# A hybrid decoder layer on one core: two token tiles come channel-major by layout, and the small constants come in three arrays

## The chip, the cores and the metric

The kernel runs on one core of one Trainium2 chip. A core has a matrix engine (TensorE, PE in the profile, with its weight loads shown as PEld), a vector engine (VectorE, DVE), a scalar engine (ScalarE, ACT), GpSimd (POOL) and SyncE (SP), which here issues most of the DMA transfers. The metric is the device time of one execution in microseconds, lower is better; times before are the median of 3 runs.

## The reference, cut to what matters

One decoder layer over 512 tokens of 1024 channels: a root-mean-square norm, a projection to queries, keys, values, a gated convolution's input and two gates, sliding-window attention, the convolution module, a merge, and a squared-ReLU MLP with 4096 hidden channels.

```python
def rms_norm(x, g):
    xf = x.astype(jnp.float32)
    y = xf * lax.rsqrt(jnp.mean(xf * xf, axis=-1, keepdims=True) + EPS)
    return (y * g.astype(jnp.float32)).astype(x.dtype)
...
        u = rms_norm(x, norm_mix_g[l])
        proj = u @ w_in[l]
        q = proj[..., :Q_END].reshape(b, s, N_Q_HEADS, HEAD_DIM)
        k = proj[..., Q_END:K_END].reshape(b, s, N_KV_HEADS, HEAD_DIM)
        v = proj[..., K_END:V_END].reshape(b, s, N_KV_HEADS, HEAD_DIM)
        glu_in = proj[..., V_END:GLU_END]
...
        attn = sliding_window_attention(q, k, v, attn_sinks[l], rel_bias) @ w_attn_o[l]
        conv = conformer_conv(glu_in, w_dw[l], b_dw[l], conv_ln_g[l], conv_ln_b[l], w_conv_out[l])
        merged = jax.nn.sigmoid(gate_attn) * attn + jax.nn.sigmoid(gate_conv) * conv
        x = x + merged @ w_out[l]
        hmid = jnp.square(jax.nn.relu(rms_norm(x, norm_mlp_g[l]) @ w_ff1[l]))
        x = x + hmid @ w_ff2[l]
```

The change concerns the first norm, `u`, and how the small constants (the norm gains of q and k, the sinks, the bias buckets, the convolution's taps, bias and norm) reach the chip.

## The kernel before

Every product is made of three matmuls in a reduced format: each operand is split into a high part (ACT casts it) and a low part (DVE or POOL subtracts the high part from the original), and high times high, high times low and low times high are summed in PSUM. All products need the activations with channels on partitions, so `u` is kept as `uTh` and `uTl`, 128 channels by 8 groups by 512 tokens.

The 512 tokens are four tiles of 128. For each tile the start of the program does this: SP loads x with tokens on partitions; ACT squares it with a running sum and takes the root (`x_square`, L294 to L297); DVE makes the reciprocal with one correction step (`rsqrt_root`, L125 to L131) and scales x by it and by the gain `gmix` in one pass (`x_scale`, L300); PE transposes the result in eight 128x128 pieces through the identity into two PSUM banks (`x_trans`, which calls `transpose_split`, L201); from each bank ACT casts the high part (L209) and DVE subtracts for the low part (L210). Then come the tile's k projection (`k_proj`) and v projection (`v_proj`), each 16 matmuls with the high weights (L316, L317) and 8 with the low ones (L320), with ACT evacuating k and its squares (L279, L281), and ACT and DVE splitting v (L333, L335). PSUM has two banks in turn for these sums (tag `mm`), two for transposes (tag `tr`) and two of tag `s`.

The order of all this is written out by hand at the end of the function (the block under `manual_schedule`): each engine executes its instructions in the order in which they stand there, and waits at an instruction whose operands are not ready with everything behind it queued. Between the tiles the first two weight chunks of the convolution's input are split (`split_hi` on ACT, L462; `split_lo` on POOL, L466). What comes after is a list of events with due positions, sorted once; `columns` (at position -2) is its first.

`columns` takes the convolution's constants: 34 rows of 1024 (31 taps, bias, norm gain, norm bias) loaded as rows, transposed on PE in eight pieces into one PSUM bank (L361), then copied on DVE to `wcol`, one column of 34 per channel and group, with the taps and the norm constants halved. It also makes the table of the relative bias with one small matmul (L363). The small constants come with nine loads of their own, issued by SP after the four tiles of x (L257 to L265).

[...] `raw_g` and `raw_a` are the first weight chunks of the convolution's input, in two buffers taken over from the raw weights of k and v.

Of the kernel before, what the change touches and what calls it, by code (L numbers as in the profile page):

```python
# [53 lines left out]
def tile_hybrid_block(  # L54
    ctx: ExitStack,
    tc: tile.TileContext,
    x: bass.AP,
    norm_mix_g: bass.AP,
    w_in: bass.AP,
    q_norm_g: bass.AP,  # L60
    k_norm_g: bass.AP,
    attn_sinks: bass.AP,
    rel_bias: bass.AP,
    w_attn_o: bass.AP,
    w_dw: bass.AP,
    b_dw: bass.AP,
    conv_ln_g: bass.AP,
    conv_ln_b: bass.AP,
# [5 lines left out]
    onehot: bass.AP,  # L74
# [24 lines left out]
    def bc(ap, n):  # L99
        return ap.partition_broadcast(n)  # L100
# [156 lines left out]
    nc.sync.dma_start(gq, bc(q_norm_g[0], P))  # L257
# [6 lines left out]
    nc.sync.dma_start(rb, rel_bias)
    nc.sync.dma_start(oh, onehot)  # L265
# [28 lines left out]
    def x_square(t, ss):  # L294
        us[t] = att.tile([P, D], F32, name=f"u_{t}", tag="pt", bufs=3)
        se.activation(us[t], xt[t], AF.Square, accum_out=ss)
        se.activation(root[t], ss, AF.Sqrt, scale=1.0 / D, bias=epsc)  # L297
# [54 lines left out]
    NR = CW + 3  # L352
    wcol = whole_lines(keep, P, KD * NR, "wcol").rearrange("p (k n) -> p k n", n=NR)
# [4 lines left out]
    def columns():  # L358
        wc_ps = ps1.tile([P, KD, NR], F32, name="wc_ps", tag="s")
        for k in range(KD):  # L360
            pe.transpose(wc_ps[:, k, :], rows[0:NR, k * P:(k + 1) * P], ident[0:NR, 0:NR])  # L361
# [3 lines left out]
        ve.tensor_copy(wcol, wc_ps)  # L365
# [1094 lines left out]
```

## Time and profile before

| | |
|---|---|
| median of 3 runs | 758.08 us (757.91 to 758.11) |
| the profiled execution | 757.91 us, its span 756.1 us |
| granted TensorE clock | 0.999 |
| PE busy | 750.6 us (99% of the span), 4474 instructions |
| DVE busy | 606.0 us (80%) |
| ACT busy | 441.3 us (58%) |
| POOL busy | 273.4 us (36%) |
| the first weights' products after the norm (`ps_g`) start | 38.10 us |

The span runs from the first to the last instruction; the measured time is 1.8 us longer. A row of a timeline or chain gives the start, the length, and the line with its operation; "x8" means eight records merged into one row; an f32 matmul that is not a transpose leaves two records. "[1.70 <-PE tp_u L207]" is idle time of that engine ahead of the row and what ended it.

### The profile page before, as it was taken

How to read it: one execution, taken by the hardware profiler on the slowest of the kernel's cores; microseconds unless marked ns; L12 is line 12 of the kernel's file. 1: busy time of each engine (PE TensorE's matmuls, PEld its weight loads, DVE VectorE, ACT ScalarE, POOL GpSimd, SP SyncE). 2: the span in 40 equal slices, each digit the busy share in tenths (PEclk: the TensorE clock that was granted, in tenths of full speed). 3: DMA queues.
4: the chain of work that ended last, by engine and by line, in shares of the span. 5: the costliest groups of instructions: out<-in, count | busy, mean ns of one | idle time of the engine just before them, and what ended most of it. 6: DMA issues, size and time to landing. Idle time of an engine off the chain costs nothing.

```text
span 756.1 us, 11678 instructions
## 1 busy us (share of the span) xinstructions
PE 750.6 (99%) x4474; PEld 663.6 (88%) x4474; DVE 606.0 (80%) x928; ACT 441.3 (58%) x697; POOL 273.4 (36%) x214
## 2 busy tenths in 40 slices
PE   9999999999999999999999999999999999999997
PEld 8989989898888888888888899988998899889986
DVE  5466998789878988878346679899879987998795
ACT  7445457757666665339235357864676467636861
POOL 1453968948774566443531002210121012101210
PEclk9999999999999999999999999999999999999999
DMA  7441040312314113531338205983498349834772
GB/s 262 149 161 56 1 168 15 126 56 81 115 61 137 56 55 112 168 111 56 112 111 294 97 29 91 263 198 117 127 230 200 112 123 228 203 116 115 171 162 111
DMA packets 66014, 97.48 MB, mean 129 GB/s; under 512 B 3540, under 2 KB 36612, under 8 KB 65958
## 3 DMA queue, kind: packets, MB, share of 16 engines
q1 hardware_dynamic: 56710, 78.91, 31.2%
q0 software_dynamic: 9248, 17.83, 13.4%
q8 instruction: 35, 0.57, 0.3%
q14 instruction: 21, 0.17, 0.1%
HBM read 94.60 MB, written 2.12 MB: 128 GB/s over the span
## 4 chain that ended last, share of the span: by engine, by line
PE 98%; DVE 2%; issue 0%; POOL 0%; DVEq 0%; POOLq 0%
PE ps_x L1177 12%; PE ps_z L1182 12%; PE ps_y L1182 6%; PE ps_y L1177 6%; PE ps_z L1177 3%; PE ps_x L1182 3%; PE ps_g L498 2%; PE ps_q L197 2%; PE ps_q L198 2%; PE ps_q L199 2%; PE ps_a L498 2%; PE ps_ta L498 2%; PE ps_a L500 2%; PE ps_g L500 2%; PE ps_g L499 2%; PE ps_ta L500 2%
## 5 line engine op out<-in xcount | busy, mean ns | idle before, releaser
L1148 DVE TENSOR_TENSOR piecel<-block,pieceh 128x1024 fp32r<-128x1024 f32 x112 | 135.7, 1219 | 27.8 <-ACT pieceh L1145 27.6
L1145 ACT CAST pieceh<-block 128x1024 fp32r<-128x1024 f32 x112 | 116.7, 1050 | 67.5 <-DVE block L1138 21.7
L803 DVE SCALAR_TENSOR_TENSOR cv<-h,wcol,cv 128x512 f32<-128x512 f32 x208 | 146.2, 746 | 0.5
L1124 POOL DMA_DIRECT2D block<-in_w_ff_dram x34 | 41.3, 1241 | 287.3 <-DVE piecel L1148 157.1
L1177 PE MATMUL ps_x<-xSh,pieceh 128*128 128x256 f32 x192 | 53.0, 276 | 0.0
L1177 PE MATMUL ps_x<-xSl,pieceh 128*128 128x256 f32 x192 | 53.0, 276 | 0.0
L1177 PE MATMUL ps_x<-xSh,piecel 128*128 128x256 f32 x192 | 53.0, 276 | 0.0
L711 ACT ACTIVATE s<-s,negm 128x257 f32<-128x257 f32 (+1 forms) x64 | 30.4, 479 | 16.0 <-DVE negm L703 16.0
L1182 PE MATMUL ps_z<-piecel,aSh 128*128 128x512 f32 (+1 forms) x98 | 37.9, 387 | 0.0
L1182 PE MATMUL ps_z<-pieceh,aSh 128*128 128x512 f32 (+1 forms) x98 | 37.7, 385 | 0.0
L1182 PE MATMUL ps_z<-pieceh,aSl 128*128 128x512 f32 (+1 forms) x98 | 37.7, 385 | 0.0
L1138 DVE TENSOR_TENSOR block<-block,block 128x1024 f32<-128x1024 f32 x30 | 36.5, 1221 | 0.8 <-DMA block<-in_w_ff_dram 0.4
L795 POOL TENSOR_TENSOR side<-side,tap 128x512 f32<-128x512 f32 x24 | 31.2, 1298 | 15.1 <-ACT tap L794 15.1
L197 PE MATMUL ps_q<-wh_q,uTh 128*128 128x256 f32 x128 | 36.5, 285 | 0.0
L199 PE MATMUL ps_q<-wh_q,uTl 128*128 128x256 f32 x128 | 36.2, 283 | 0.0
L198 PE MATMUL ps_q<-wl_q,uTh 128*128 128x256 f32 x128 | 36.2, 283 | 0.0
L1177 PEld LDWEIGHTS ps_x<-xSh,piecel 128*128 128x128 f32 x192 | 36.0, 188 | 0.0
L1177 PEld LDWEIGHTS ps_x<-xSh,pieceh 128*128 128x128 f32 x192 | 36.0, 188 | 0.0
L1177 PEld LDWEIGHTS ps_x<-xSl,pieceh 128*128 128x128 f32 x192 | 36.0, 188 | 0.0
L735 DVE TENSOR_TENSOR pTl<-ptp,pTh 128x512 fp32r<-128x512 f32 x28 | 19.0, 686 | 17.8 <-ACT pTh L731 17.8
L720 POOL TENSOR_TENSOR s<-s,r 128x1024 f32<-128x1024 f32 (+1 forms) x16 | 26.9, 1684 | 16.7 <-DVE r L715 16.7
L1216 ACT CAST aSh<-c 128x1024 fp32r<-128x1024 f32 x16 | 16.8, 1053 | 21.4 <-DVE c L1230 11.7
(325 smaller groups left out, 2531.8 us busy)
## 6 DMA issues: line engine op xcount, KB each, us to landing
block<-in_w_ff_dram SPq DMA_DIRECT2D x64, 512.0 KB, 5.5
block<-in_w_ff_dram POOLq DMA_DIRECT2D x34, 512.0 KB, 6.9
x<-in_x_dram SPq DMA_DIRECT2D x8, 512.0 KB, 4.2
raw_g<-in_w_in_dram SPq DMA_DIRECT2D x8, 512.0 KB, 4.4
raw_a<-in_w_in_dram SPq DMA_DIRECT2D x8, 512.0 KB, 3.5
raw_q<-in_w_in_dram SPq DMA_DIRECT2D x8, 512.0 KB, 4.5
raw_ta<-in_w_in_dram SPq DMA_DIRECT2D x8, 512.0 KB, 4.3
raw_tc<-in_w_in_dram SPq DMA_DIRECT2D x8, 512.0 KB, 3.5
```

What stands on the lines that cost most here:

```text
L197: pe.matmul(ps, ah, wh, start=first, stop=False)
L198: pe.matmul(ps, ah, wl, start=False, stop=False)
L199: pe.matmul(ps, al, wh, start=False, stop=last)
L498: pe.matmul(ps, wh[:, k, :], ah(k), start=(k == 0), stop=False)
L500: pe.matmul(ps, wl[:, k, :], ah(k), start=False, stop=(k == KD - 1))
L803: ve.scalar_tensor_tensor(out=cps[ct], in0=src, scalar=w, in1=cps[ct], op0=ALU.mult, op1=ALU.add)
L1124: ge.dma_start(tl["raw"][buf][:, ks, :], block(ph, i, j)[:, ks, :], accum_op=ALU.add)
L1138: ve.tensor_tensor(out=o, in0=a, in1=b, op=ALU.add)
L1145: se.copy(piece("h", n), tl["raw"][buf][:, 2 * h:2 * h + 2, :])
L1148: ve.tensor_tensor(out=piece("l", n), in0=tl["raw"][buf][:, 2 * h:2 * h + 2, :], in1=piece("h", n).bitcast(F32), op=ALU.subtract)
L1177: pe.matmul(o, b[:, c, w], a[:, k, :], start=(first and c + q + i == 0), stop=(k == 3 and i == 2), skip_group_check=True)
L1182: pe.matmul(acc[:, cols], a[:, k, w], b[:, c, cols], start=(first and c + i == 0), stop=(k == 3 and i == 2), skip_group_check=True)
```

## The change

Four things change.

1. Token tiles 2 and 3 are loaded twice. The host lays out a second copy of these 256 tokens, `x_cols`, with 128 channels on partitions and 8 groups by 128 tokens behind each. The token-major copy is now only squared and summed (in place); the other one, `xc`, becomes `u`: DVE multiplies by the gain, which lies one per channel and group in `gcol` (`cols_gain`); PE spreads the tokens' 128 reciprocal roots to all partitions with one f32 matmul per tile (`cols_spread`: the factors as a broadcast stationary operand, the identity as the moving one) into `rsb`; DVE multiplies by `rsb` in two halves into PSUM; ACT casts each half to the high part and DVE subtracts for the low part (`cols_split`). Tiles 0 and 1 go on as before.
2. The convolution's constants and `gcol` come as columns in one array `channels` (35 columns by 8 groups for each partition), so the eight transposes and a copy in `columns` go; DVE's halving works in place.
3. The gains of q and k and the sinks come as one broadcast load, `vectors`, and the bias table with its one-hot matrix as one, `buckets`. Nine small loads become three; two large ones are new.
4. The order at the start is written anew around these steps; SP issues the two small arrays behind `raw_g`.

```diff
@@ -245,24 +240,19 @@
     vw_raw = wp.tile([P, KD, 256], F32, name="raw_v", tag="raw", bufs=2)
     load_kv(vw_raw, K_END, 0)
     load_kv(vw_raw, K_END, 1)
+    NR = CW + 3
+    flat = whole_lines(keep, P, KD * (NR + 1), "wcol")
+    wcol = flat[:, 0:KD * NR].rearrange("p (k n) -> p k n", n=NR)
+    gcol = flat[:, KD * NR:KD * NR + KD]
     xt += [load_x(2), load_x(3)]
-
-    rows = att.tile([P, D], F32, name="rows", tag="qraw", bufs=2)
-    rb_sink = whole_lines(keep, P, LINE // 4, "rb_sink")
-    rb = rb_sink[0:32, 16:16 + NQ]
-    oh = sm.tile([32, P], F32, name="oh", tag="osb", bufs=1)
-    gq = keep.tile([P, HD], F32, name="gq")
-    gk = keep.tile([P, HD], F32, name="gk")
-    nsink = rb_sink[:, 32:32 + NQ]
-    nc.sync.dma_start(gq, bc(q_norm_g[0], P))
-    nc.sync.dma_start(gk, bc(k_norm_g[0], P))
-    nc.sync.dma_start(nsink, bc(attn_sinks[0], P))
-    nc.sync.dma_start(rows[0:CW, :], w_dw[0])
-    nc.sync.dma_start(rows[CW:CW + 1, :], b_dw)
-    nc.sync.dma_start(rows[CW + 1:CW + 2, :], conv_ln_g)
-    nc.sync.dma_start(rows[CW + 2:CW + 3, :], conv_ln_b)
-    nc.sync.dma_start(rb, rel_bias)
-    nc.sync.dma_start(oh, onehot)
+    nc.sync.dma_start(flat[:, 0:KD * (NR + 1)], channels)
+    xc = {t: att.tile([P, KD, P], F32, name=f"xc_{t}", tag="qraw", bufs=2) for t in (2, 3)}
+    for t in (2, 3):
+        nc.sync.dma_start(xc[t], x_cols[t - 2].rearrange("p (k c) -> p k c", c=P))
+    vecs = whole_lines(keep, P, 3 * LINE // 4, "vecs")
+    gq, gk, nsink = vecs[:, 0:HD], vecs[:, HD:2 * HD], vecs[:, 2 * HD:2 * HD + NQ]
+    bucket = sm.tile([32, NQ + P], F32, name="bucket", tag="osb", bufs=1)
+    rb, oh = bucket[:, 0:NQ], bucket[:, NQ:NQ + P]
 
 
     uTh = keep.tile([P, KD, S], F32R, name="uTh", tag="act", bufs=2)
...
@@ -292,7 +282,7 @@
     us = {}
 
     def x_square(t, ss):
-        us[t] = att.tile([P, D], F32, name=f"u_{t}", tag="pt", bufs=3)
+        us[t] = xt[t] if t in xc else att.tile([P, D], F32, name=f"u_{t}", tag="pt", bufs=3)
         se.activation(us[t], xt[t], AF.Square, accum_out=ss)
         se.activation(root[t], ss, AF.Sqrt, scale=1.0 / D, bias=epsc)
 
...
@@ -301,6 +291,26 @@
 
     def x_trans(t):
         transpose_split(ps1, (us[t][:, 0:S], us[t][:, S:D]), uTh, uTl, t, f"u{t}")
+
+    rsb = {}
+
+    def cols_gain(t):
+        ve.tensor_tensor(out=xc[t], in0=xc[t], in1=gcol.unsqueeze(2).to_broadcast([P, KD, P]), op=ALU.mult)
+
+    def cols_spread(t, rs):
+        rsb[t] = ps1.tile([P, P], F32, name=f"rsb_{t}", tag="s")
+        pe.matmul(rsb[t], rs.to_broadcast([P, P]), ident, start=True, stop=True)
+
+    def cols_split(t):
+        for half in range(2):
+            ks, cols = slice(4 * half, 4 * half + 4), slice(t * P, (t + 1) * P)
+            u = ps1.tile([P, 4, P], F32, name=f"uc_{t}{half}", tag="tr")
+            ve.tensor_tensor(out=u, in0=xc[t][:, ks, :], in1=rsb[t].unsqueeze(1).to_broadcast([P, 4, P]), op=ALU.mult)
+            se.copy(uTh[:, ks, cols], u)
+            us[t, half] = u
+        for half in range(2):
+            ks, cols = slice(4 * half, 4 * half + 4), slice(t * P, (t + 1) * P)
+            ve.tensor_tensor(out=uTl[:, ks, cols], in0=us[t, half], in1=uTh[:, ks, cols].bitcast(F32), op=ALU.subtract)
 
     def hi_lo(dst, raw, j, hi_fn, lo_eng):
         ks = slice(4 * j, 4 * j + 4)
...
@@ -349,22 +359,16 @@
         events.append((pos, len(events), fn, args))
 
 
-    NR = CW + 3
-    wcol = whole_lines(keep, P, KD * NR, "wcol").rearrange("p (k n) -> p k n", n=NR)
     lnh = eps_ln[:, 16:16 + KD * 2].rearrange("p (k n) -> p k n", n=2)
     rel = att.tile([NQ, 3 * P], F32, name="rel", tag="bias")
     rel_d = dr.tile([NQ, 3 * P], F32, name="rel_d")
 
     def columns():
-        wc_ps = ps1.tile([P, KD, NR], F32, name="wc_ps", tag="s")
-        for k in range(KD):
-            pe.transpose(wc_ps[:, k, :], rows[0:NR, k * P:(k + 1) * P], ident[0:NR, 0:NR])
         rel_ps = ps1.tile([P, P], F32, name="rel_ps", tag="s")
         pe.matmul(rel_ps[0:NQ, :], rb, oh, start=True, stop=True)
         ve.memset(rel, NEG)
-        ve.tensor_copy(wcol, wc_ps)
-        ve.tensor_scalar(out=wcol[:, :, 0:CW], in0=wc_ps[:, :, 0:CW], scalar1=0.5, scalar2=None, op0=ALU.mult)
-        ve.tensor_scalar(out=lnh, in0=wc_ps[:, :, CW + 1:CW + 3], scalar1=0.5, scalar2=None, op0=ALU.mult)
+        ve.tensor_scalar(out=wcol[:, :, 0:CW], in0=wcol[:, :, 0:CW], scalar1=0.5, scalar2=None, op0=ALU.mult)
+        ve.tensor_scalar(out=lnh, in0=wcol[:, :, CW + 1:CW + 3], scalar1=0.5, scalar2=None, op0=ALU.mult)
         ve.tensor_copy(rel[:, P:2 * P], rel_ps[0:NQ, :])
         nc.sync.dma_start(rel_d, rel)
 
...
@@ -1384,6 +1388,8 @@
         vlo1()
         load(1)
         x_square(2, ss2[:, 0:1])
+        nc.sync.dma_start(vecs[:, 0:2 * HD + NQ], bc(vectors[0], P))
+        nc.sync.dma_start(bucket, buckets)
         vp = v_proj(0)
         next(vp)
         x_trans(1)
...
@@ -1392,23 +1398,25 @@
         rs2 = rsqrt_root(roots[:, 2:4], mean_eps(ss2, D, 2, "x23"), 2, "x23")
         ksum()
         next(vp)
-        x_scale(2, rs2[:, 0:1])
+        cols_gain(2)
         ksum = k_proj(1)
+        for t in (2, 3):
+            cols_spread(t, rs2[:, t - 2:t - 1])
+        cols_split(2)
         vp = v_proj(1)
         next(vp)
-        x_trans(2)
         split_hi(0)
         split_lo(0)
-        x_scale(3, rs2[:, 1:2])
+        cols_gain(3)
         ksum()
         for _ in vp:
             pass
         split_hi(1)
         split_lo(1)
+        cols_split(3)
         ksum = k_proj(2)
         vp = v_proj(2)
         next(vp)
-        x_trans(3)
         split_hi(2)
         split_lo(2)
         ksum()
...
@@ -1447,9 +1455,16 @@
     from concourse.bass_utils import run_bass_kernel_spmd as _run
 
     nc = _bacc.Bacc("TRN2", target_bir_lowering=False, num_devices=1, dynamic_dma_scratch_size=2048)
+    packed = dict(inputs)
+    packed["x_cols"] = inputs["x"][0, 2 * P:].reshape(2, P, KD, P).transpose(0, 3, 2, 1).reshape(2, P, D)
+    packed["vectors"] = _np.concatenate([inputs[n] for n in ("q_norm_g", "k_norm_g", "attn_sinks")], axis=1)
+    packed["buckets"] = _np.concatenate([inputs["rel_bias"], _bucket_onehot()], axis=1)
+    rows = _np.concatenate([inputs["w_dw"][0]] + [inputs[n] for n in ("b_dw", "conv_ln_g", "conv_ln_b")])
+    packed["channels"] = _np.concatenate([rows.reshape(CW + 3, KD, P).transpose(2, 1, 0).reshape(P, KD * (CW + 3)),
+                                          inputs["norm_mix_g"].reshape(KD, P).T], axis=1)
     arrays, args = {}, []
-    for name in _INS + ["onehot"]:
-        a = _bucket_onehot() if name == "onehot" else _np.ascontiguousarray(inputs[name])
+    for name in _INS:
+        a = _np.ascontiguousarray(packed[name])
         arrays[f"in_{name}_dram"] = a
         args.append(nc.dram_tensor(f"in_{name}_dram", a.shape, _mybir.dt.from_np(a.dtype), kind="ExternalInput").ap())
     args.append(nc.dram_tensor("out_0_dram", _OUT, _mybir.dt.float32, kind="ExternalOutput").ap())
```

The places where the order of instructions differs are these. First PE, from the end of tile 1's k projection to the start of tile 2's k projection (`ps_v` is tile 1's v, `tp_u` are the transposes of tile 2; "..." stands for alternating rows of the same sum). Before:

```order
L320 MATMUL ps_k_305<-kw_153,uTh 128x256 x8
L316 MATMUL ps_v_333<-vw_154,uTh 128x256
...
L207 MATMUL tp_u_0_350<-ident,u_249 128x128 x4
L207 MATMUL tp_u_1_357<-ident,u_249 128x128 x4
L320 MATMUL ps_v_333<-vw_155,uTh 128x256 x8
L316 MATMUL ps_k_384<-kw_152,uTh 128x256
```

And with the change:

```order
L330 MATMUL ps_k_298<-kw_147,uTh 128x256 x8
L302 MATMUL rsb_326<-ident,roots 128x128
L302 MATMUL rsb_328<-ident,roots 128x128
L326 MATMUL ps_v_338<-vw_148,uTh 128x256
...
L330 MATMUL ps_v_338<-vw_149,uTh 128x256 x8
L326 MATMUL ps_k_383<-kw_146,uTh 128x256
```

The transposes inside tile 1's v projection are gone (and likewise those inside tile 2's), and two small matmuls stand ahead of it.

Second DVE, from tile 0's v part to tile 1's v part (`u_249` is the scaled tile 2, `u_283` tile 3; `xc_133` and `xc_134` are the channel-major tiles 2 and 3, `uc` the PSUM halves). Before:

```order
L335 TENSOR_TENSOR vv<-ps_v_252,vv 128x4x64
L300 SCALAR_TENSOR_TENSOR u_249<-x_127,roots,gmix 128x1024
L210 TENSOR_TENSOR uTl<-tp_u_0_350,uTh 128x4x128
L210 TENSOR_TENSOR uTl<-tp_u_1_357,uTh 128x4x128
L300 SCALAR_TENSOR_TENSOR u_283<-x_129,roots,gmix 128x1024
L282 TENSOR_REDUCE ssk<-sq 128x4
L335 TENSOR_TENSOR vv<-ps_v_333,vv 128x4x64
```

And with the change:

```order
L345 TENSOR_TENSOR vv<-ps_v_246,vv 128x4x64
L298 TENSOR_TENSOR xc_133<-xc_133,wcol 128x1024
L308 TENSOR_TENSOR uc_330<-xc_133,rsb_326 128x512
L308 TENSOR_TENSOR uc_333<-xc_133,rsb_326 128x512
L313 TENSOR_TENSOR uTl<-uc_330,uTh 128x4x128
L313 TENSOR_TENSOR uTl<-uc_333,uTh 128x4x128
L298 TENSOR_TENSOR xc_134<-xc_134,wcol 128x1024
L272 TENSOR_REDUCE ssk<-sq 128x4
L345 TENSOR_TENSOR vv<-ps_v_338,vv 128x4x64
```

Each scaling has become a gain multiplication and two scalings of a half; tile 3's gain multiplication stands where its scaling stood. On ACT the casts of tile 3's high parts have moved ahead of the evacuation of tile 2's k and stay behind the cast of `wh_a`.

Third SP, from the last tile of x to `raw_a`. Before:

```order
L231 DMA x_129<-in_x_dram 128x1024
L257 DMA gq<-in_q_norm_g_dram 128x64
...
L264 DMA rb_sink<-in_rel_bias_dram 32x16
L265 DMA oh<-in_onehot_dram 32x128
L449 DMA raw_g_180<-in_w_in_dram 128x4x256 x2
L449 DMA raw_a_246<-in_w_in_dram 128x4x256 x2
```

And with the change:

```order
L226 DMA x_130<-in_x_dram 128x1024
L248 DMA wcol<-in_channels_dram 128x280
L251 DMA xc_133<-in_x_cols_dram 128x1024
L251 DMA xc_134<-in_x_cols_dram 128x1024
L453 DMA raw_g_173<-in_w_in_dram 128x4x256 x2
L1391 DMA vecs<-in_vectors_dram 128x144
L1392 DMA bucket<-in_buckets_dram 32x144
L453 DMA raw_a_239<-in_w_in_dram 128x4x256 x2
```

The nine small loads are gone from ahead of `raw_g`, and three others, two of them of 512 KB, stand there.

More of the change, by code (lines that the diff above doesn't have):

```diff
@@ L57, in tile_hybrid_block @@
     x: bass.AP,
+    x_cols: bass.AP,
     norm_mix_g: bass.AP,
     w_in: bass.AP,
[L60 to L63, printed above, removed]
+    vectors: bass.AP,
+    buckets: bass.AP,
+    channels: bass.AP,
     w_attn_o: bass.AP,
[L65 to L68, printed above, removed]
     w_conv_out: bass.AP,
@@ L73, in tile_hybrid_block @@
     w_ff2: bass.AP,
-    onehot: bass.AP,
     out: bass.AP,
@@ L1421, in tile_hybrid_block @@
             fn(*args)
-_INS = ["x", "norm_mix_g", "w_in", "q_norm_g", "k_norm_g", "attn_sinks", "rel_bias", "w_attn_o", "w_dw", "b_dw",
-        "conv_ln_g", "conv_ln_b", "w_conv_out", "w_out", "norm_mlp_g", "w_ff1", "w_ff2"]
+_INS = ["x", "x_cols", "norm_mix_g", "w_in", "vectors", "buckets", "channels", "w_attn_o", "w_conv_out", "w_out",
+        "norm_mlp_g", "w_ff1", "w_ff2"]
 _OUT = (S, D)
```

## The prediction

> **What bounds the kernel now.** I read the page first: busy times, then the engines of the chain that ended last.
>
> ```profile
> span 756.1 us, 11678 instructions
> PE 750.6 (99%) x4474; PEld 663.6 (88%) x4474; DVE 606.0 (80%) x928; ACT 441.3 (58%) x697; POOL 273.4 (36%) x214
> PE 98%; DVE 2%; issue 0%; POOL 0%; DVEq 0%; POOLq 0%
> ```
>
> The matmul engine is busy for all but 5.5 us, and it is 98% of the chain. Then the waits of PE over the whole span, which are one line:
>
> ```profile
> PE warm L225 <- POOL eps_ln L122: 1.5, 1, 1.5
> ```
>
> So a microsecond of PE work that is taken away anywhere after the start is a microsecond off the end, as long as nothing PE reads comes later than PE wants it. Both halves of the question lie in the stretch that the change rewrites, so the third view is the chain between 20 and 39 us, in order of time (start, length, what; the first row is from the same view of an earlier stretch):
>
> ```profile
> 9.59 0.89 PE warm L225 x8
> ...
> 20.74 0.12 PE ps_v L316
> ...
> 22.66 0.87 PE tp_u L207 x8
> 23.53 0.95 PE ps_v L320 x8
> 24.59 0.29 PE ps_k L317
> ...
> 26.56 0.96 PE ps_k L320 x8
> ...
> 29.44 0.87 PE tp_u L207 x8
> 30.31 0.95 PE ps_v L320 x8
> 31.37 0.29 PE ps_k L317
> ...
> 33.33 0.96 PE ps_k L320 x8
> 34.29 0.12 PE ps_v L316
> ...
> 36.21 0.96 PE ps_v L320 x8
> 37.17 0.61 PE wc_ps L361 x8
> 37.78 0.32 PE rel_ps L363 x2
> 38.10 0.43 PE ps_g L498
> ```
>
> The page calls PE busy here, yet two short waits hide in it. Undisturbed, the 16 matmuls of a token tile's first part take 34.29 to 36.21, that is 1.92 us. The k projection of tile 2 takes 24.48 (the end of the row at 23.53) to 26.56, 2.08 us; that of tile 3 31.26 to 33.33, 2.07 us. Each waits some 0.15 us in its first `uTl` matmul (the 0.29 us rows).
>
> **The change part by part: PE.** Removed: the two transposes of tiles 2 and 3, 0.87 us each, 1.74 us; the eight transposes of the constants' rows, 0.61 us. Removed if the new operands come in time: the two hidden waits, 0.16 + 0.15 = 0.31 us. Added: two f32 matmuls of 128 columns that spread the tokens' factors over all partitions. The nearest row is the warm-up, four such matmuls (eight records) in 0.89 us, 0.22 each, so 0.45 us for both. From below they cost what two single 128-column transposes do, 2 x 0.87 / 8 = 0.22 us, from above what `rel_ps` takes including the switch of operands, 2 x 0.32 = 0.64 us. I take the warm-up, the same instruction and shape. Walked forward from 20.74: factors 21.19, v of tile 1 to 24.07 (1.92 + 0.96), k of tile 2 to 26.95, v to 29.83, k of tile 3 to 32.71, v to 35.59, `rel_ps` to 35.91, where the first `ps_g` starts; before it started at 38.10. **The sum is -1.74 - 0.61 - 0.31 + 0.45 = -2.2 us**, with the bounds -1.7 (dear factors, waits kept) to -2.4.
>
> **VectorE, tile 2.** Before, DVE did one fused scaling per tile. Now it does a gain multiplication over 1024 elements, two scalings of 512 by the spread factor in PSUM into PSUM, then the two low parts.
>
> ```profile
> 19.43 0.16 DVE L130 SCALAR_TENSOR_TENSOR roots<-a_x,roots 128x2 f32<-128x2 f32 x1
> 20.17 1.27 DVE L300 SCALAR_TENSOR_TENSOR u<-x,roots,gmix 128x1024 f32<-128x1024 f32 x1
> 23.75 1.29 DVE L210 TENSOR_TENSOR uTl<-tp_u,uTh 128x512 fp32r<-128x512 f32 x2 [2.30 <-ACT uTh L209]
> 24.95 1.28 DVE L300 SCALAR_TENSOR_TENSOR u<-x,roots,gmix 128x1024 f32<-128x1024 f32 x1
> 42.07 1.23 DVE L390 TENSOR_TENSOR kraw<-kraw,y_k 128x1024 f32<-128x1024 f32 x1
> ```
>
> The gain is the form of L390 (a tensor times a broadcast one): 1.23. For the scaling there is the same form later, one operand and the result in PSUM, in the view that groups by shape:
>
> ```profile
> L632 DVE TENSOR_TENSOR ps_wc<-ta,ps_wc 128x512 f32<-128x512 f32 x8 | 5.6, 695 | 0.3
> ```
>
> DVE is free at 20.17, as before. Gain to 21.43; the factors were wanted on PE at 20.74 and `roots` is ready at 19.59, so PE does not wait there and DVE has them by 21.2. Scalings 21.43 to 22.13 and to 22.75; ACT's high parts (1.08 us for two, started 0.48 apart, in the rows at 23.13 and 24.09 below) 22.2 to 22.8 and 22.8 to 23.4; low parts to 23.5 and 24.1. PE's first `uTl` matmul of tile 2 is at 24.2, the fifth pair at 25.0. Margins 0.7 and 0.9 us: the waits vanish. If the scaling cost 1.0 us in place of 0.70, the margin would be gone and nothing more.
>
> **Tile 3 and the queues behind.** DVE's second gain runs 24.0 to 25.3, the sum of squares and the v part of tile 1, 256 elements each, to about 26.0 (an estimate from the 1.23 us of 1024 elements; PE wants that bank at 26.95), the scalings to 27.4. What hangs on more than DVE is ACT, which in program order must first split two weights:
>
> ```profile
> 17.32 1.07 ACT L296 ACTIVATE u<-x 128x1024 f32<-128x1024 f32 x1
> ...
> 23.13 1.08 ACT L209 CAST uTh<-tp_u 128x512 fp32r<-128x512 f32 x2 [1.70 <-PE tp_u L207]
> 24.09 1.06 ACT L462 CAST wh_g<-raw_g 128x1024 fp32r<-128x1024 f32 x1
> 26.36 1.05 ACT L462 CAST wh_a<-raw_a 128x1024 fp32r<-128x1024 f32 x1 [0.93 <-DMA raw_a<-in_w_in_dram]
> ```
>
> `wh_a` waited for its load, and now tile 3's high parts stand right behind it, with the evacuation of k behind them. From a landing at L, the cast and the high parts are done at L + 2.1; the evacuations, 256 elements each, add at most 0.6 (an estimate from the 0.48 of 512). PE wants both at 29.83, so L may be 27.1. Does it hold? SP's issues, then a transfer's time to landing, then the traffic:
>
> ```profile
> 7.54 0.90 SPq L257 DMA_DIRECT2D gq<-in_q_norm_g_dram  x1
> 16.04 0.32 SPq L264 DMA_DIRECT2D rb_sink<-in_rel_bias_dram  x1
> 20.61 0.92 SPq L449 DMA_DIRECT2D raw_a<-in_w_in_dram  x2
> ```
> ```profile
> gq<-in_q_norm_g_dram SPq DMA_DIRECT2D x1, 32.0 KB, 8.7
> ```
> ```profile
> 14.00:16.00 2.00, 2.00 (x19) 1.98 (x18) 2.00 (x3) 2.00 (x5) 0.00 (x0) 1.00 0.76 258
> 16.00:18.00 2.00, 2.00 (x18) 1.91 (x17) 1.98 (x3) 1.97 (x6) 0.00 (x0) 1.00 0.07 26
> 22.00:24.00 2.00, 2.00 (x20) 2.00 (x19) 0.25 (x1) 0.87 (x2) 0.00 (x0) 1.00 1.02 344
> 24.00:26.00 2.00, 2.00 (x18) 1.90 (x17) 2.00 (x3) 1.42 (x3) 0.77 (x1) 1.00 0.53 186
> ```
>
> (The last two columns are the share of the DMA engines and GB/s.) Nine small loads, of which the row at 16.04 is the eighth, held back the weights behind them, and from 16 to 18 the engines stood nearly idle (26 GB/s). Now two loads of 0.52 MB and one of 0.14 MB stand there, and `raw_g` follows as soon as its buffer is free. The data of the last `x` tile ended at about 15.5 (0.76 of the window from 14). From there 0.14 + 1.05 + 1.05 (`raw_g`) + 0.09 + 1.05 (`raw_a`) = 3.4 MB at the 344 GB/s of a full window end at 25.3. Before, `raw_a`'s data ended near 25.1 (0.53 of the window from 24) and the cast started at 26.36, 1.3 later; so it lands at 26.6, about as before and 0.5 us ahead of need. The channel-major tile 2 lands near 18.6, and is needed at 20.17. These loads cost nothing; that cover is the second thing to watch. The constants that now come as columns save DVE one copy and their landing is long before use; the merged small arrays free SP. All of that is at zero, hidden behind PE.
>
> After 38 us both programs run the same work in the same order, and every producer starts from a PE result or from a buffer PE or POOL frees, so I let the rest shift as a whole. The profiled execution took 757.91 us, 1.8 around its span of 756.1; its median sibling 758.08. I expect a span of 753.9 and **755.9 us** for the median.
>
> **Rivals.**
>
> *DVE loses a race with POOL (757.7).* Two rows of DVE and POOL that overlap:
>
> ```profile
> 93.06 2.41 POOL L466 TENSOR_TENSOR wl_g<-raw_g,wh_g 128x1024 fp32r<-128x1024 f32 x1
> ```
> ```profile
> 93.50 3.05 DVE L561 TENSOR_TENSOR qs<-qraw,qs 128x1024 fp32r<-128x1024 f32 x1
> ```
> ```profile
> 25.23 3.27 POOL L466 TENSOR_TENSOR wl_g<-raw_g,wh_g 128x1024 fp32r<-128x1024 f32 x1 [13.86 <-ACT wh_g L462]
> ```
>
> A DVE operation on two SBUF tensors that meets a running POOL one ended 1.08 us after it (96.55 against 95.47): it had waited it out. At 25.23 POOL came second, behind the scaling at 24.95, and took 0.86 longer than the 2.41 of the other row. The second gain is such an operation, and `wl_g` is issued just there. By the walk DVE starts it at 24.0 and POOL is ready at 24.4, both counted from the same ACT cast, so DVE wins by 0.4 us. If it loses, the gain ends at 24.4 + 2.41 + 1.23 = 28.0 instead of 25.3, the v part of tile 1 at 28.75, and PE, which has the next projection queued behind that bank, stands 1.8 us: -0.4 in all. [...]
>
> *Tile 3 of x lands late (757.4).* PE now wants the factors at 20.74, two microseconds before it wanted their product. If the new loads share the engines with the last `x` load instead of following it, that lands up to 1.2 MB / 344 GB/s = 3.5 us later, at 19.5. The factors follow their tile's square by 2.3 us (17.32 to 19.59), so they come at 21.8; PE stands 1.0 us there and 0.5 at tile 2's low part, -0.7 in all. Against it: the small load issued at 7.54 landed 8.7 us later, at 16.24, just after the `x` load (16.04, when SP's next issue was let go). [...]
>
> *The added traffic holds back `raw_a` (slower: 760).* From L = 27.1 on each microsecond of it is one of PE, through ACT's order. At -2.2 it takes L = 29.3 to reach the old time and 30.8 to be slower by a measurable amount; at a mean rate of 230 GB/s the data end at 30.2 and land at 31.5, which gives +4.4 - 2.2 = +2.2, 760 us. For it: 1.2 MB more in the busiest stretch. Against it: the window of `raw_g` and `raw_a` that is full runs at 344.
>
> *Given back later (757.0).* The shift may not stay rigid, since DVE and POOL meet often (L561), and a DVE operation held for 2 us can make PE wait once; half the gain gone.
>
> **Chances.** Forecast 0.74 (own range 755.5 to 756.4), lost race 0.08, late `x` 0.05, given back 0.05, late `raw_a` 0.08 (a quarter of it so little that the time stays within no change). A measurement of this kernel tells 0.2%, 1.5 us, from nothing, so the border of faster is 756.56: the forecast lies beyond it, three rivals within no change, one mostly slower: 0.74, 0.20, 0.06. Range 755.4 to 757.7, which leaves out the slow case and the edges.
>
> **What would show it.** Right: `ps_g` first at 35.9 (35.6 to 36.4), no `tp_u` for tiles 2 and 3, two `rsb` matmuls of 0.4 to 0.6 us together, the k projections of tiles 2 and 3 at 2.88 us each. A lost race shows as a second gain of 3 us or more and a hole ahead of tile 2's v projection; late loads as ACT waiting for `raw_a` beyond 27.1, or PE waiting in front of `rsb`. If `ps_g` is at 35.9 and the end is not 2.2 us earlier, the rigid shift was the wrong step.

## The result, and the profile after

The changed kernel took 755.61 us (median of 7 runs, 755.41 to 756.5), the kernel before 757.99 (757.37 to 758.59) beside it: a ratio of 0.9969, 95% interval 0.9959 to 0.9978. The forecast was 755.9. The page of the changed kernel, then the waits of PE over its whole span (total, times, longest):

```profile
span 753.7 us, 11633 instructions
PE 747.8 (99%) x4454; PEld 661.0 (88%) x4454; DVE 607.7 (81%) x931; ACT 440.4 (58%) x697; POOL 272.9 (36%) x214
```
```profile
PE warm L220 <- POOL eps_ln L117: 1.5, 1, 1.5
PE ps_k L327 <- DVE uTl L205: 0.2, 1, 0.2
```

PE's busy time fell by 2.8 us, with 20 matmul records fewer, and the span by 2.4. After its start PE waits once, 0.2 us in tile 0's k projection, ahead of the rewritten stretch. The chain of the changed kernel in the stretch that was rewritten (start, length, what):

```profile
19.58 0.96 PE ps_k L330 x8
20.53 0.44 PE rsb L302 x4
20.98 0.12 PE ps_v L326
...
22.89 0.96 PE ps_v L330 x8
23.85 0.12 PE ps_k L326
...
25.77 0.96 PE ps_k L330 x8
...
28.65 0.96 PE ps_v L330 x8
...
31.53 0.96 PE ps_k L330 x8
...
34.41 0.96 PE ps_v L330 x8
35.37 0.32 PE rel_ps L368 x2
35.69 0.43 PE ps_g L502
```

From the end of tile 1's k (20.53) to the first `ps_g` it is 15.16 us; before, 20.74 to 38.10, it was 17.36. **The difference is 2.20 us.** Every projection now takes 2.88 us (25.77 to 28.65, and so on): the two hidden waits are gone. The other 0.21 us lie ahead of 20.53, where the changes below scatter as much (20.4 to 21.1 in the runs below that leave the start as it is). From `ps_g` to the end of the span both kernels take 718.0 us (756.1 - 38.10, 753.7 - 35.69).

The changed kernel's timelines of DVE, ACT and POOL (start, length; in brackets idle time ahead and what ended it):

```profile
19.95 1.22 DVE L298 TENSOR_TENSOR xc<-xc,wcol 128x1024 f32<-128x1024 f32 x1
21.27 1.29 DVE L308 TENSOR_TENSOR uc<-xc,rsb 128x512 f32<-128x512 f32 x2
22.62 1.29 DVE L313 TENSOR_TENSOR uTl<-uc,uTh 128x512 fp32r<-128x512 f32 x2
23.83 1.22 DVE L298 TENSOR_TENSOR xc<-xc,wcol 128x1024 f32<-128x1024 f32 x1
```
```profile
22.00 1.18 ACT L309 CAST uTh<-uc 128x512 fp32r<-128x512 f32 x2 [0.78 <-DVE uc L308]
...
25.72 1.05 ACT L466 CAST wh_a<-raw_a 128x1024 fp32r<-128x1024 f32 x1 [1.31 <-DMA raw_a<-in_w_in_dram]
26.68 1.06 ACT L309 CAST uTh<-uc 128x512 fp32r<-128x512 f32 x2
```
```profile
24.21 3.11 POOL L470 TENSOR_TENSOR wl_g<-raw_g,wh_g 128x1024 fp32r<-128x1024 f32 x1 [12.74 <-ACT wh_g L466]
```

DVE's second gain starts 0.38 us ahead of POOL's `wl_g`, which pays for it (3.11 us in place of 2.41); `raw_a` is cast from 25.72 on. The traffic of the changed kernel (a row gives the window, its length, the busy time of PE, PEld, DVE, ACT and POOL with their instructions, then the granted clock, the share of the DMA engines, and GB/s):

```profile
16.00:18.00 2.00, 2.00 (x18) 1.84 (x17) 2.00 (x3) 2.00 (x4) 0.00 (x0) 1.00 1.01 406
...
22.00:24.00 2.00, 2.00 (x19) 2.00 (x18) 1.94 (x4) 1.99 (x3) 0.00 (x0) 1.00 0.87 306
24.00:26.00 2.00, 2.00 (x19) 2.00 (x19) 2.00 (x4) 0.69 (x3) 1.79 (x1) 1.00 0.05 16
```

The stretch from 16 to 18, which stood nearly idle before (26 GB/s), is full, and the data end about 24.

### The profile page after: what moved, and what is told of

It reads as the page before. It is cut to its first block, busy times and chain, and to the rows that moved or that the text cites. A ratio compares the mean times of both kernels' runs of the same rounds, so it can differ in the third digit from the quotient of the medians.

```text
span 753.7 us, 11633 instructions
## 1 busy us (share of the span) xinstructions
PE 747.8 (99%) x4454; PEld 661.0 (88%) x4454; DVE 607.7 (81%) x931; ACT 440.4 (58%) x697; POOL 272.9 (36%) x214
## 3 DMA queue, kind: packets, MB, share of 16 engines
q0 software_dynamic: 9248, 17.83, 13.5%
## 4 chain that ended last, share of the span: by engine, by line
PE 96%; DVE 1%; DMA 1%; ACT 0%; issue 0%; SPq 0%; DVEq 0%
PE ps_x L1181 11%; PE ps_z L1186 11%; PE ps_y L1181 6%; PE ps_y L1186 5%; PE ps_z L1181 3%; PE ps_x L1186 3%; PE ps_g L502 2%; PE ps_q L192 2%; PE ps_q L194 2%; PE ps_q L193 2%; PE ps_a L502 2%; PE ps_ta L502 2%; PE ps_a L504 2%; PE ps_g L504 2%; PE ps_g L503 2%; PE ps_a L503 2%
## 5 line engine op out<-in xcount | busy, mean ns | idle before, releaser
L1152 DVE TENSOR_TENSOR piecel<-block,pieceh 128x1024 fp32r<-128x1024 f32 x112 | 135.9, 1222 | 29.8 <-ACT pieceh L1149 29.7
L799 POOL TENSOR_TENSOR side<-side,tap 128x512 f32<-128x512 f32 x24 | 31.0, 1291 | 15.2 <-ACT tap L798 15.2
L1220 ACT CAST aSh<-c 128x1024 fp32r<-128x1024 f32 x16 | 16.8, 1053 | 24.1 <-DVE c L1234 12.6
```

The source lines that it names most:

```text
L799: ge.tensor_tensor(out=side[ct], in0=side[ct], in1=tap, op=ALU.add)
L1152: ve.tensor_tensor(out=piece("l", n), in0=tl["raw"][buf][:, 2 * h:2 * h + 2, :], in1=piece("h", n).bitcast(F32), op=ALU.subtract)
```

## The experiments

The table has all kernels that were run; "from rsb" is the time from the start of the row of the spread factors (without them: of the first row of tile 1's v; with tile 3 of x behind, where PE waits ahead of this row: from where tile 1's k would have let it start, 20.39) to that of the first `ps_g` in PE's timeline, so it shows what a run lost inside the rewritten stretch, apart from what happened before it. It is 17.5 us in the kernel before and 15.2 in the changed one.

| kernel | median us (before beside it) | ratio, 95% | first `ps_g` | from rsb |
|---|---|---|---|---|
| constants only | 757.02 (758.22) | 0.9983, 0.9973 to 0.9993 | 37.20 | 16.8 |
| tiles only | 759.34 (758.22) | 1.0015, 1.0006 to 1.0025 | 40.01 | 19.7 |
| tiles only, small loads last | 756.15 (758.17) | 0.9976, 0.9967 to 0.9985 | 36.26 | 15.9 |
| tiles only, hole filled | 758.32 (758.17) | 1.0002, 0.9993 to 1.0011 | 39.23 | 18.7 |
| second gain late | 757.58 (758.22) | 0.9992, 0.9983 to 1.0001 | 37.58 | 17.2 |
| second gain first (control) | 755.62 (758.22) | 0.9964, 0.9951 to 0.9977 | 36.02 | 15.2 |
| one more load | 755.60 (758.31) | 0.9962, 0.9949 to 0.9974 | 35.97 | 15.2 |
| three more loads | 758.40 (758.31) | 1.0003, 0.9994 to 1.0013 | 37.90 | 16.9 |
| x tile 3 behind | 756.76 (758.31) | 0.9981, 0.9972 to 0.999 | 36.94 | 16.5 |
| three tiles | 760.85 (758.31) | 1.0033, 1.002 to 1.0046 | 38.95 | 15.2 |
| gain as a row | 757.88 (758.17) | 0.9994, 0.9985 to 1.0003 | 38.13 | 15.2 |
| gain as a row, warmed up | 757.47 (758.11) | 0.9991, 0.9982 to 1.0001 | 36.90 | 15.2 |

The theory was the prediction's: the gain is PE work, and each cover has the margin that was worked out. The rivals were its four.

### The change in two halves

Constants only: the arrays and the columns, with tiles 2 and 3 token-major as before.

```diff
-        cols_gain(2)
+        x_scale(2, rs2[:, 0:1])
         ksum = k_proj(1)
-        for t in (2, 3):
-            cols_spread(t, rs2[:, t - 2:t - 1])
-        cols_split(2)
...
+        x_trans(2)
```

> The constants as columns and in three arrays, tiles 2 and 3 token-major as before the change. Theory (PE's work is the price, term by term): only the eight transposes of the constants' rows go, 0.61 us; the first ps_g starts at 37.5 instead of 38.10, the span is 755.5, the time 757.4. Rival (the arrays themselves matter, since SP is free earlier and raw_g and raw_a come sooner): more than 0.61 us, up to the 2.4 us of the whole change. Rival (the gain comes from the tiles alone): 758.0.

From the end of tile 1's k to `ps_g` it is 16.75 us against 17.36: 0.61, the eight transposes to the hundredth. The median fell by 1.20 and not by 0.61 (the interval allows 0.5 to 2.0); of the 1.2 us by which the profiled spans differ, 0.3 lie ahead of the stretch and 0.3 behind `ps_g`, and no run tells these from scatter.

Tiles only: the channel-major tiles, with nine small loads behind them and the constants' transposes on PE.

```diff
     for t in (2, 3):
         nc.sync.dma_start(xc[t], x_cols[t - 2].rearrange("p (k c) -> p k c", c=P))
+    nc.sync.dma_start(gq, vectors[0, 0:HD].partition_broadcast(P))
+    nc.sync.dma_start(gk, vectors[0, HD:2 * HD].partition_broadcast(P))
...
+    nc.sync.dma_start(oh, buckets[:, NQ:NQ + P])
...
+        for k in range(KD):
+            pe.transpose(wc_ps[:, k, :], rows[0:NR, k * P:(k + 1) * P], ident[0:NR, 0:NR])
```

> Tiles 2 and 3 channel-major, but the constants as rows with their eight transposes, and the nine small loads ahead of raw_g (with one more for the gain's columns). Theory (PE's work alone): -1.74 - 0.31 + 0.45 = -1.6 us, the first ps_g at 36.5, 756.4. Rival (the three arrays are needed, since SP's order holds raw_g and raw_a back behind ten small loads and two large ones): raw_a lands at 27 to 28 instead of 25.7, ACT's cast of it holds up tile 3's high parts, PE stands up to 1 us: ps_g at 37 to 37.5, 757.0 to 757.4.

This was **slower than the kernel before**, where the rival had 757.0 to 757.4. SP's issues, ACT, and PE's waits with its matmuls behind the hole, in the run with the tiles only:

```profile
10.49 0.33 SPq L259 DMA_DIRECT2D gq<-in_vectors_dram  x1
11.81 0.33 SPq L260 DMA_DIRECT2D gk<-in_vectors_dram  x1
...
18.62 0.54 SPq L267 DMA_DIRECT2D oh<-in_buckets_dram  x1
19.26 0.95 SPq L469 DMA_DIRECT2D raw_g<-in_w_in_dram  x2
```
```profile
26.86 1.04 ACT L482 CAST wh_g<-raw_g 128x1024 fp32r<-128x1024 f32 x1 [3.78 <-DMA raw_g<-in_w_in_dram]
27.81 0.37 ACT L355 CAST vv<-ps_v 128x256 fp32r<-128x256 f32 x1
```
```profile
28.68 0.41 PE L338 MATMUL ps_v<-vw,uTh 128*128 128x256 f32 x1 [2.07 <-DVE vv L357]
28.91 0.40 PE L339 MATMUL ps_v<-vw,uTl 128*128 128x256 f32 x1
29.11 0.41 PE L338 MATMUL ps_v<-vw,uTh 128*128 128x256 f32 x1
...
32.09 1.23 PE L342 MATMUL ps_v<-vw,uTh 128*128 128x256 f32 x8
```

While the large loads ahead of them move, SP lets go of most of the small ones 1.2 to 1.4 us apart (the one at 18.26 waits for the landing of `xc`, at 18.24; in the kernel before, where they also stand 1.2 to 1.4 us apart from 9.59 to 16.04, SP's waits name the landings of earlier loads of `raw_k`, `raw_v` and `x`, 0.7 to 1.1 us each), so `raw_g` is issued at 19.26 (12.64 in the changed kernel) and lands at 26.8. ACT stands at `wh_g`, the cast of tile 1's v stands behind it, and PE waits 2.07 us for its bank. Then something that no step had: the 16 matmuls take 3.41 us (28.68 to 32.09) in place of 1.92. They start 0.21 apart where it was 0.12. The granted clock (third column from the end) in that stretch:

```profile
28.00:30.00 2.00, 1.32 (x7) 1.32 (x8) 1.62 (x3) 0.67 (x2) 2.00 (x1) 0.73 0.11 37
30.00:32.00 2.00, 2.00 (x11) 2.00 (x11) 0.93 (x2) 2.00 (x6) 1.73 (x2) 0.50 0.00 0
```

It is 0.50. The hole of 2.07 us costs 1.49 more in matmuls at half speed. Of the 3.8 us that this run lost against the two tiles without a wait (19.7 - 15.9), these two are 3.56.

Not every execution pays the second part. Of the ten, six have a mean granted clock of 0.997 or 0.998 and a median of 759.9, and the profiled one is among them; four have 1.00 and a median of 758.5, which is not clear of the kernel before (758.22, from 757.75 to 759.12). The 1.4 us between the two groups are of the size of the 1.49 above.

Two runs take the two causes apart. First, the same kernel with the nine loads written behind `raw_a` (in SP's rows two of them still go ahead of it, at 13.56 and 14.70, and seven behind):

```diff
         load(1)
+        nc.sync.dma_start(gq, vectors[0, 0:HD].partition_broadcast(P))
...
+        nc.sync.dma_start(oh, buckets[:, NQ:NQ + P])
         x_square(2, ss2[:, 0:1])
```

> The tiles alone, with the constants still in nine loads of their own and their eight transposes on PE, but the nine loads issued behind raw_a instead of ahead of raw_g. If it was only their place in front of raw_g that made the tiles alone slower: raw_g is issued near 10.5 and cast by 23, PE has no wait, ps_g starts at the changed kernel's 35.7 plus 0.61 for the transposes = 36.3, 756.3 us in all. If the loads cost by their number wherever they stand (SP's later issues, other loads' landings): PE still waits for vv or raw_a, ps_g at 38 or later, 758 us or more.

`ps_g` starts at 36.26 and the time is 756.15, both as expected: the place of the nine loads was all of it, and not their number. From the end of tile 1's k to `ps_g` it is 15.77 us against 17.36, so the tiles alone are worth 1.59; with the 0.61 of the constants this is the 2.20 of the whole change. Second, the tiles alone with matmuls put into the hole:

```diff
+        for _ in range(8):
+            pe.matmul(fill, ident, ident, start=True, stop=True)
         next(vp)
```

> The tiles alone as run before, with eight more f32 matmuls of 128 columns (0.22 us each, 1.78 in all; their result is not used) put on PE between tile 2's k and v projections, into the hole of 2.07 us that the late raw_g makes there. If the halved clock behind that hole (0.50 from 30 to 32, matmuls 0.21 apart instead of 0.12, some 1.45 us in all) comes of PE standing idle: the hole stays, the clock stays at 1.00, ps_g at 40.0 - 1.45 = 38.6, 757.9 us, faster by more work. If the clock does not depend on the idle time: the row of 0.21 stays, ps_g at 40.0 and 759.3; if the fill itself delays v: up to 1.8 more.

PE and the granted clock of the filled run:

```profile
26.62 1.95 PE L1435 MATMUL fill<-ident 128*128 128x128 f32 x16
28.85 0.39 PE L338 MATMUL ps_v<-vw,uTh 128*128 128x256 f32 x1 [0.27 <-DVE vv L357]
```
```profile
30.00:32.00 2.00, 1.97 (x17) 1.76 (x15) 0.77 (x2) 2.00 (x5) 1.73 (x2) 1.00 0.03 8
```

The clock stays at 1.00, and all ten executions have a mean of 0.999 or 1.00, so here the fall came of PE's idle time. The stretch got 1.0 us shorter and not 1.45: PE then waited 0.3 us ahead of tile 3's k for ACT, which was held up by `raw_a` (cast at 29.67), and the first matmul behind that wait took 0.38 us in place of 0.12. Without the fill, what is missing from 1.00 between 28 and 34 (0.73 and 0.50, then 0.92 from 32 to 34) adds up to 1.70 us, that is 3.4 us at 0.50. A gap of 2.07 us was followed by this fall in the profiled execution; one of 1.7 us (below) was not. Four of the ten executions of the tiles alone show no fall; their gaps were not profiled, but the 1.4 us between the two groups leave little room for shorter ones. Where the border lies, and whether the length of a gap alone draws it, is open.

### The race between DVE and POOL

Second gain late: one extra scaling of 512 elements ahead of the second gain, repeated into tile 2's PSUM bank, which nobody reads afterwards, so that POOL starts first. The control has the same extra work behind the gain.

```diff
+        again = us[2, 0]
+        ve.tensor_tensor(out=again, in0=xc[2][:, 0:4, :], in1=rsb[2].unsqueeze(1).to_broadcast([P, 4, P]), op=ALU.mult)
         cols_gain(3)
```

> The changed kernel with one more DVE operation (tile 2's first scaling repeated into its PSUM bank, 0.69 us) ahead of the second gain multiplication, so that this is ready 0.2 us after POOL's wl_g instead of 0.4 before it. Theory (a DVE operation on two SBUF tensors and a POOL one exclude each other): the gain takes 3 us and ends near 27.9, the v part of tile 1 near 28.6, PE stands 1.8 us ahead of tile 2's v projection: ps_g at 37.5, 757.4. Rival (no exclusion, 0.69 us more on DVE fits into its margin): ps_g at 35.7, 755.6.

> The control to the run with the late gain: the same additional DVE operation, but behind the second gain multiplication, so that DVE still comes first. Theory (it is the order of DVE and POOL, not DVE's work): no loss, ps_g at 35.7, 755.6. Rival (0.69 us more on DVE is itself too much there): a wait of PE at tile 2's v projection, 36.0 or later.

DVE, POOL, PE's wait and the granted clock behind it, gain late:

```profile
24.37 3.28 DVE L298 TENSOR_TENSOR xc<-xc,wcol 128x1024 f32<-128x1024 f32 x1
```
```profile
24.16 2.41 POOL L470 TENSOR_TENSOR wl_g<-raw_g,wh_g 128x1024 fp32r<-128x1024 f32 x1 [12.74 <-ACT wh_g L466]
```
```profile
PE ps_v L326 <- DVE vv L345: 1.7, 1, 1.7
```
```profile
28.00:30.00 2.00, 1.63 (x13) 1.64 (x14) 1.95 (x4) 1.04 (x2) 1.89 (x1) 1.00 0.00 0
```

The gain came 0.21 us behind POOL and ended 1.08 after it (27.65 against 26.57), the same 1.08 as in the prediction's rows. Inside the stretch 2.0 us are lost (17.2 - 15.2) where 1.8 were reckoned, and 757.58 stands against the rival's 757.7. The granted clock held at 1.00 behind this hole, and no execution of the ten has a mean below 0.999. In the control nothing is lost, and its extra scaling, which has one operand in SBUF and one in PSUM, ran its normal 0.69 us beside POOL's `wl_g`: only the operation with two SBUF operands was held up.

### How much later `raw_a` may come

One or three more loads of 512 KB, of data that is not used, issued ahead of `raw_a` (in SP's rows the two small arrays then go behind it).

```diff
+        nc.sync.dma_start(more0, x_cols[0].rearrange("p (k c) -> p k c", c=P))
...
         load(1)
```

> The changed kernel with one more load of 512 KB (never read) ahead of raw_a. Theory (raw_a's landing L sets ACT's cast, and from L = 27.0 on PE waits; it is 25.7 in the changed kernel): at 390 GB/s it comes 1.35 us later, 27.1, PE loses 0.1: ps_g at 35.8, 755.7. Rival (the added traffic costs from the first byte): 1.35 us, 757.0.

> The changed kernel with three more loads of 512 KB (never read) ahead of raw_a. Theory (from a landing at 27.0 each microsecond is one of PE): L = 25.7 + 4.0 = 29.7, PE stands 2.7 us ahead of tile 3's k projection: ps_g at 38.4, 758.3, the whole gain and a little more given back. Rival (loads are hidden anyway): ps_g at 35.7, 755.6.

ACT with one more load, then ACT and PE's wait with three:

```profile
26.89 1.05 ACT L467 CAST wh_a<-raw_a 128x1024 fp32r<-128x1024 f32 x1 [2.18 <-DMA raw_a<-in_w_in_dram]
```
```profile
28.93 1.05 ACT L469 CAST wh_a<-raw_a 128x1024 fp32r<-128x1024 f32 x1 [3.96 <-DMA raw_a<-in_w_in_dram]
```
```profile
PE ps_k L329 <- ACT sq L271: 1.4, 1, 1.4
```

The prediction put the border at 27.1, with a microsecond of PE for each one beyond. At 26.89 nothing is lost. At 28.93, 1.8 us beyond, the stretch is 1.7 longer, and PE waits for ACT's evacuation of k behind tile 3's casts, as the step said. The landing was 0.8 us sooner than the 29.7 expected, and the loss smaller by 1.0 (1.7 for 2.7). The profiled execution took 757.9; that the median, 758.40, met the 758.3 of the expectation is luck. Five of the ten executions have a mean clock of 0.999 and a median of 757.9, the other five 0.996 or 0.997 and 759.5: a fall of the clock, which no step had, added some 1.6 us to them. None of these five was profiled, so the holes ahead of their falls are not known; in the profiled one PE waits 1.41 us and the clock stays at 1.00.

### Tile 3 of x late

The token-major tile 3 is issued behind the new loads, which makes the roots late.

```diff
-    xt += [load_x(2), load_x(3)]
+    xt.append(load_x(2))
...
+    xt.append(load_x(3))
```

> The changed kernel with the last token-major tile loaded behind the columns and the two channel-major tiles. Theory (PE wants the factors at 20.5, so this load has a deadline of its own): it lands 1.2 MB / 390 GB/s = 3.1 us later, near 19.1, the factors come at 21.4, PE stands 0.9 us ahead of rsb and 0.4 at tile 2's low part: ps_g at 37.0, 756.9. Rival (the factors have slack): ps_g at 35.7, 755.6.

PE waits of this run:

```profile
PE rsb L303 <- DVE roots L125: 0.5, 1, 0.5
```

The stretch is 1.24 us longer (16.48 against 15.24): 0.5 as the wait ahead of the factors, and the rest in short pieces around and behind them (0.27 in tile 2's k projection). The prediction's rival had 1.0 and 0.5, from a landing at 19.5 that it took from 344 GB/s; here ACT has the tile near 18.7 (an estimate: DVE takes its sum of squares at 19.90, and in the changed kernel at 18.30 for a square from 17.11 on).

### Going further

Three tiles: tile 1 comes channel-major as well, which takes another 0.87 us of transposes off PE.

```diff
-        x_scale(1, rsqrt_root(root[1], mean_eps(ss1, D, 1, "x1"), 1, "x1"))
+        rs1 = rsqrt_root(root[1], mean_eps(ss1, D, 1, "x1"), 1, "x1")
         vlo0()
+        cols_gain(1)
         vlo1()
...
-        x_trans(1)
+        cols_spread(1, rs1)
+        cols_split(1)
```

> Tile 1 channel-major too, its load and the columns ahead of the token-major tiles 2 and 3. Theory (the change pays only where DVE, DMA and ACT have room): PE saves 0.87 - 0.22 = 0.65 us more, but tile 1's load lands near 15.1, its gain multiplication stands on DVE ahead of the second half of v's low weights, and its low parts come near 19.5 where PE wants them at 17.7: ps_g at 37.5, 757.4, slower than the changed kernel by 1.8. Rival (the more tiles, the better): ps_g at 35.0, 754.9.

PE's waits in the three tiles, then the granted clock:

```profile
PE ps_v L332 <- DVE vw L320: 1.1, 1, 1.1
...
PE ps_k L328 <- ACT uTh L311: 0.5, 1, 0.5
PE ps_k L329 <- DVE uTl L315: 0.3, 1, 0.3
```
```profile
20.00:22.00 2.00, 2.00 (x11) 2.00 (x11) 1.45 (x8) 0.81 (x4) 0.00 (x0) 0.50 1.09 381
```

The waits add up to 1.9 us, of the size of the loss that was expected; but they stand within 3 us, and the granted clock falls to 0.50 for 3.4 us behind them too (0.79, 0.50 and 0.86 from 18 to 24, 1.70 us missing from 1.00; a mean of 0.997 or 0.998 in four of five executions). With it tile 1's k ends 3.3 us later than in the changed kernel (23.80 against 20.53). A further 1.3 us of waits stand far behind, at `ps_z`, for the MLP's weights: 1.0 for DVE's low parts and 0.3 for ACT's high part. Why these are late is open; two other runs (small loads last, three more loads) wait 0.4 us at the same place.

Gain as a row: the broadcast load of the token-major gain (512 KB) becomes one row of 4 KB, which PE spreads over the partitions with two f32 matmuls of one stationary row; the warm-up is shortened to make room.

```diff
-    warm_up(WARM)
...
+    nc.sync.dma_start(line, norm_mix_g)
...
-    nc.sync.dma_start(gmix, bc(norm_mix_g[0], P))
...
+        warm_up(5)
+        for h in range(2):
+            pe.matmul(gmix[h], one, line[:, h * S:(h + 1) * S], start=True, stop=True)
+        warm_up(4)
```

> The changed kernel with the token-major gain (a broadcast load of 512 KB ahead of nearly everything) replaced by a row of 4 KB, which PE spreads over the partitions into two PSUM banks with two f32 matmuls; the warm-up is shortened for it, and tiles 0 and 1 are scaled in two halves from there. If the prologue is bound by its loads: all the early ones come about 1.3 us sooner (0.52 MB at 410 GB/s), ps_g at 34.6, 754.6 us. If it is bound by ACT and DVE between the loads (casts of the first weights, roots, scalings): ps_g at 35.7 and 755.6; the two halves cost DVE about 0.15 us more per tile, so up to 0.3 later is possible too.

The first weights were cast at 6.20 in place of 7.95, so the loads did come sooner. PE ran everything up to 13.5 at half speed (matmuls 0.21 apart in place of 0.12; the column of the granted clock does not show it, it reads 1.00 during the slow start of the changed kernel too), and tile 1's k ended 2.45 us later than in the changed kernel. The second form keeps a longer warm-up ahead of the spread:

```diff
-        warm_up(5)
+        warm_up(11)
...
-        warm_up(4)
```

> The run before this one (gain as a row, spread by PE) with eleven full warm-up matmuls ahead of the two spreading ones in place of five ahead and four behind. There PE ran everything up to 13.5 us at half speed, so although the first weights were cast 1.75 us sooner, tile 0's transposes and k projection came later. If that half speed was the shortened warm-up: the clock is up by 5.2 us as in the changed kernel (its 40 warm-up records take 6.46 us, which is 14 or 15 at the 0.25 us seen with five matmuls in 2.5 us and the rest at 0.11), the spread ends near 7.8, the transposes' rows take 0.87 and not 1.7 us, k of tile 1 ends by 20.1 to 20.4, ps_g at 35.2 to 35.5, 755.1 to 755.4. If the spread itself, which uses one row of the array, lets the clock fall or not rise: transposes at 1.7 us again, ps_g at 37 or later, 757 and more.

PE, then the granted clock, of this run:

```profile
1.47 4.66 PE L222 MATMUL warm<-ident 128*128 128x128 f32 x22 [1.47 <-POOL eps_ln L119]
6.06 1.98 PE L1380 MATMUL gmix<-gmix_row,eps_ln 1*128 1x512 f32 x4
8.41 1.68 PE L204 MATMUL tp_u<-ident,u 128*128 128x128 f32 x8 [0.38 <-DVE u L294]
```
```profile
8.00:10.00 2.00, 1.62 (x10) 1.44 (x10) 1.23 (x3) 0.59 (x1) 2.00 (x1) 0.74 1.07 385
10.00:12.00 2.00, 2.00 (x11) 2.00 (x11) 1.39 (x3) 1.87 (x3) 0.00 (x1) 0.50 1.09 419
```

The warm-up was enough: the spread ran at full speed (1.98 us; the first form took 3.78). Yet the clock fell behind it, with only 0.38 us of idle time in between: by the 0.74 of the window from 8 to 10 it fell near 9.0, in the middle of the transposes, whose row takes 1.68 us against 1.08 in the changed kernel, and stayed at 0.50 for 3.4 us (0.74, 0.50 and 0.91 from 8 to 14, 1.70 us missing from 1.00). So the rival holds as far as the fall goes: matmuls of one row, 1.98 us that the profile calls busy, stood where the kernel before has full ones. Whether they, the 0.38 us or the transposes brought the fall is not shown: no run has full matmuls in the place of the spread. This run also waits 1.2 us at `ps_z`, as the three tiles do. Neither form beats the changed kernel, and no run here does beyond its interval.

## Why the prediction was right

The time was 755.61 for 755.9, and by its own steps:

- **The sum of PE work** (-1.74 - 0.61 - 0.31 + 0.45 = -2.2): 2.20 from tile 1's k to `ps_g`. The constants' part alone measured 0.61, the two factors 0.44 (0.45 was taken from the warm-up), and the hidden waits are gone. The price of the spread between its bounds of 0.22 and 0.64 was the warm-up's, as chosen.
- **`ps_g` at 35.9**: 35.69. The sum was exact; the 0.2 us more lie ahead of the rewritten stretch and are luck, since the runs scatter there by 0.7.
- **VectorE, tile 2**: low parts done at 23.9, forecast 24.1; PE took them without a wait. The scaling with PSUM on both sides took 0.69 us on average, as its row of before said (0.70).
- **The lost race**: DVE was ahead by 0.38 us (forecast 0.4), and the run that turns the order over cost what the rival named. The chance of 0.08 was a chance on 0.4 us of margin, and it was real: an extra operation of 0.69 us is enough.
- **The landing of `raw_a`**: 26.6 forecast, 25.7 measured. The step mis-sized the rate: it took the 344 GB/s of one full window of before, while the full windows from 14 to 22 now moved 376 to 414. The need at 27.1 was right, so the margin is 1.4 us and not 0.5.
- **"All of that is at zero, hidden behind PE"** (the loads and the merged arrays): true of the sum, and the weakest sentence of the prediction. Priced alone, the new loads without the merged arrays turn the gain of 1.6 us into a loss of 1.1 in the median (759.34 against 758.22), some of it by the clock of six executions in ten. Where the small loads stand is worth 3.2 us to this change (759.34 against 756.15). The step looked at the new loads with the small ones already gone and did not ask what each does without the other.
- **The late `raw_a`, slower** and **tile 3 of x late**: both mechanisms work as written, and their points of decision were right or close; neither was reached.
- **The rigid shift**: 718.0 us behind `ps_g` in both kernels.

What the prediction had nowhere is the price of a longer hole: every wait in it was costed at its own length. For a hole of 1.7 us the runs bear this out; at 2.07 us in one piece the bill was 3.56 in the profiled execution, and with three more loads half of the executions paid for the clock as well.

## What to carry to other kernels

Here, where PE never waited, removed PE work was worth its own duration, 2.20 us for a sum of 2.2 made from single rows; what needs the care are the covers, each with the moment at which it is needed and at which it comes. Price each part of a change without the others as well: a part that costs nothing may be what keeps another from costing. And count holes together: a wait of 2.07 us on the matmul engine cost 1.49 more in clock in the profiled execution, and six of ten executions show a fall, so look at the clock of each and not only at the median. Here eight full matmuls in the hole, whose result nobody reads, kept it at 1.00.

## What the runs showed of the hardware

- **The granted clock fell to 0.50** for 3.4 us after PE stood idle for 2.07 us in one piece (in six of ten executions by their mean clock), and after 1.9 us of waits in three pieces within 3 us (four of five); it did not after 1.7 us (none of ten). Eight f32 matmuls filled into the hole kept it at 1.00 in all ten.
- It also fell, for as long, after 1.98 us of f32 matmuls with one stationary row, 0.38 us of idle time and half a microsecond of transposes; from 8 to 10 the profile calls PE busy for 1.62 of 2 us. Which of these brought the fall is not shown.
- **Small loads behind large ones** were mostly let go 1.2 to 1.4 us apart on SP while the large ones moved (five of the eight steps from 10.49 to 18.62 with the tiles only): with nine of them ahead of it, `raw_g` was issued 6.6 us later than in the changed kernel (19.26 against 12.64).
- **Two SBUF operands**: a DVE operation of 1.22 us took 3.28 where POOL began 0.21 us sooner, and POOL's took 3.11 in place of 2.41 where DVE was first. One with an operand and the result in PSUM kept its 0.69 us beside POOL.
- DMA moved 376 to 414 GB/s in the four 2 us windows from 14 to 22 of the changed kernel; in the kernel before it moved 344 from 22 to 24.
